# Storing two heads at a time, 64 KB per partition, in a batched Q K^T kernel

## The chip, the cores and the metric

The kernel runs on one core of a Trainium2 chip. The metric is the device time of one execution in microseconds (us). The core has a matrix engine (TensorE, PE in the profile, its weight loads PEld), VectorE (DVE), ScalarE (ACT), GpSimd (POOL) and SyncE (SP, which here only issues transfers). Sixteen transfer engines move data between the main memory (HBM) and the on-chip memory (SBUF, 128 partitions). Transfers are issued by SP (queue q1 of the profile) and by ScalarE (q10), and all of them share the sixteen engines. A transfer is made of packets; each engine closes its part of a transfer with a 4-byte record. TensorE writes only to PSUM, from where ScalarE or VectorE copies to SBUF.

## The reference

For 8 x 12 = 96 heads, each with Q and K of 1024 rows by 64 columns in f32, the kernel computes all products of a row of Q with a row of K:

```python
batch, n_heads, seq, head_dim = 8, 12, 1024, 64
np.einsum('bhid,bhjd->bhij', q, k).astype(np.float32)
```

One head's result is 1024 x 1024 f32, 4 MiB; all 96 are 402.65 MB. Q and K together are 50.33 MB. No softmax and no scaling follow.

## The kernel before

**Blocks.** The 96 heads are cut into blocks of 2, 2, 4, 8, 8 and then six of 12 heads (`sizes`, L33). A block's Q and K are loaded, cast to f16, transposed so that the head dimension lies on the partitions, and then multiplied head by head. All of the work is written in one program order per engine (`pin`), so that each engine's queue runs in the order of the code; engines wait for each other by data only.

**Loads.** For the first three blocks the raw input goes into the first half of what is later an output buffer, `early` (32 KB per partition). From the fourth block on, each block's Q and K go into two buffers of `in_pool` (L73). `next_load` takes the next of these from the list `stream`: two at the start, the rest on ScalarE's queue, both of a block together, after the second eviction of one head of the block two before it (`LOADS`, L263: head 1 of block 2, head 4 of blocks 3 and 4, head 6 otherwise). A load waits until POOL has cast what was in its buffer.

**Cast.** POOL casts f32 to f16 in chunks (`cast_quads`, L127), four instructions of 32 partitions per chunk, into one of five buffers of `half_pool`; `CHUNK` bounds a chunk's columns. Blocks of 8 heads give eight chunks of 1024 columns, blocks of 12 eight chunks of 1536. The first two blocks are cast by `cast_rows` (L97).

**Transpose.** VectorE transposes each chunk in blocks of 32 x 32 into `qT` and `kT` (L145). The first half of a block's heads lies on partitions 0 to 63, the second half on 64 to 127; head n uses half `n // (N/2)` and column group `g = n % (N/2)`. The transposes of the next block are spread over the heads of the present one (`side`), two buffers each of `qT` and `kT` alternate. The first two blocks are transposed by TensorE (L151, copied out at L154).

**Scores.** For one head (`scores`, L156), TensorE multiplies 128 rows of Q by 512 rows of K at a time, over the 64 partitions of the head's half (L171). Row `8 p + t` of the head comes out on partition p for the t-th of eight groups, so that each partition holds eight whole rows of the result, 32 KB that are contiguous in HBM. Two PSUM buffers of 2048 columns alternate; ScalarE copies each to the output buffer (L181), four copies per head; only the first head has copies of 1024 columns, half of them on VectorE (L179). SP then stores the head in one transfer of 4 MiB (L185). There are three output buffers (`out_pool`, L45).

Of the kernel before, what the change touches and what calls it, by code (L numbers as in the profile page):

```python
# [8 lines left out]
F16 = mybir.dt.float16  # L9
F32 = mybir.dt.float32  # L10
P = 128

@with_exitstack
def kernel(
# [6 lines left out]
    nc = tc.nc  # L21

    B, H, S, D = q.shape
    NT = S // P
    BH = B * H
# [4 lines left out]
    kf = k.rearrange("b h s d -> (b h s) d")  # L30
    of = out.rearrange("b h i j -> (b h) i j")

    sizes = [2, 2, 4, 8, 8] + [12] * ((BH - 24) // 12)  # L33
    assert sum(sizes) == BH
    PE_BLOCKS = 2
    NMAX = max(sizes)
    CHUNK = 48 * 32

    consts = ctx.enter_context(tc.tile_pool(name="consts", bufs=1))
    ident = consts.tile([P, P], F16)  # L40

    in_pool = ctx.enter_context(tc.tile_pool(name="in_pool", bufs=2))
    half_pool = ctx.enter_context(tc.tile_pool(name="half_pool", bufs=5))
    tr_pool = ctx.enter_context(tc.tile_pool(name="tr_pool", bufs=2))
    out_pool = ctx.enter_context(tc.tile_pool(name="out_pool", bufs=3))  # L45

    pin = tc.keep_in_program_order

    def half_tile():
        half_sb = half_pool.tile([P, CHUNK], F16, tag="half")  # L50
        return half_sb

    class Block:
# [3 lines left out]
        def __init__(self, first, N, by_pe):  # L57
# [5 lines left out]
            self.halves = {}  # L63
            self.cut = max(1, self.R * 32 // CHUNK + (self.R * 32 % CHUNK > 0))

# [87 lines left out]
            src = t_ps.rearrange("c t m -> c m t")  # L153
            pin(copy(out=dst, in_=src))  # L154

        def scores(self, n, side, ps_pool, w):  # L156

            half, g = divmod(n, self.N // 2)
            cs = slice(half * D, (half + 1) * D)

            qT = self.qT.rearrange("c (g m t) -> c g t m", t=NT, m=P)
            kT = self.kT.rearrange("c (g j) -> c g j", j=S)
            o_sb = out_pool.tile([P, NT, S], F32, tag="out")
            for u in range(NT // w):
                ps = ps_pool.tile([P, w * S], F32, tag="po")
                for tt in range(w):
                    for j in range(2):
                        js = slice(j * 512, (j + 1) * 512)
                        at = tt * S + j * 512
                        pin(  # L170
                            nc.tensor.matmul(  # L171
                                ps[:, at : at + 512],
                                qT[cs, g, w * u + tt],
                                kT[cs, g, js],
                            )
                        )
                dst = o_sb[:, w * u : w * u + w].rearrange("p t j -> p (t j)")
                if w == 1 and u % 2:
                    pin(nc.vector.tensor_copy(out=dst, in_=ps))  # L179
                else:  # L180
                    pin(nc.scalar.copy(out=dst, in_=ps))  # L181
                for do in side.get(u, []):
                    do()
            pin(
                nc.sync.dma_start(  # L185
                    out=of[self.first + n].rearrange("(p t) j -> p (t j)", p=P),
                    in_=o_sb.rearrange("p t j -> p (t j)"),
                )
            )

    blocks, first = [], 0
    for i, N in enumerate(sizes):
        blocks.append(Block(first, N, i < PE_BLOCKS))
        first += N

    early = out_pool.tile([P, NT, S], F32, tag="out")
    raw = early.rearrange("p t j -> p (t j)")
    at = 0
    for b in blocks[:3]:
# [12 lines left out]
    def next_load(eng):  # L212
        if stream:
            b, x = stream.pop(0)
            b.load(x, eng)
# [9 lines left out]
    def to_half(last):  # L225
        while casts:
            i, c = casts[0]
            if i > last or (blocks[i], c[0]) in stream:
                return
            blocks[i].cast_quads(*c)  # L230
            casts.pop(0)

    for b in blocks[:PE_BLOCKS]:
        for x in range(2):
            b.cast_rows(x)
    to_half(2)

    def block(i, heads, ps_pool, w):
        b = blocks[i]
        nxt = blocks[i + 1] if i + 1 < len(blocks) else None  # L240
        for n in heads:
            side = {}
            if nxt and nxt.by_pe:
                if n == 1:
                    side = {
                        u: [
                            lambda x=u // 2: nxt.transpose_rows(
                                x, ps_pool, nc.vector.tensor_copy
                            )
                        ]  # L250
                        for u in (1, 3)
                    }
            elif nxt:
                parts = nxt.chunks()
                some = [s for m, s in enumerate(parts) if m * b.N // len(parts) == n]
                side = {0: [lambda s=s: nxt.transpose_quads(*s) for s in some]}

            if n == LOADS.get(i, 6):
                side[1] = side.get(1, []) + [lambda: next_load(nc.scalar)] * 2
            b.scores(n, side, ps_pool, w)  # L260
            to_half(i + 2 + (n == b.N - 1))

    LOADS = {0: None, 1: None, 2: 1, 3: 4, 4: 4}  # L263

    blocks[0].alloc()
    blocks[1].alloc()
    with tc.tile_pool(name="first_pool", bufs=4, space=bass.MemoryType.PSUM) as pool:
        for x in range(2):
            blocks[0].transpose_rows(x, pool, (nc.vector.tensor_copy, nc.scalar.copy)[x])
        block(0, [0], pool, 1)  # L270
    po_pool = ctx.enter_context(
        tc.tile_pool(name="po_pool", bufs=2, space=bass.MemoryType.PSUM)
    )
    block(0, [1], po_pool, 2)
    for i in range(1, len(blocks)):
        if i + 1 < len(blocks):
            blocks[i + 1].alloc()
        block(i, range(blocks[i].N), po_pool, 2)


# [28 lines left out]
```

## Time and profile before

| what | value |
|---|---|
| median of the runs | 1063.13 us (1063.09 to 1063.64) |
| span of the profiled execution | 1061.8 us (the median of the runs is 1.3 above it) |
| PE, DVE, ACT, POOL busy | 66%, 44%, 66%, 35% of the span |
| transfers, mean rate over the span | 453.25 MB, 427 GB/s |
| stores | 96 of 4096 KB, 21.8 us median from issue to landing |
| eviction of 128 x 2048 f32 on ScalarE | 380, 1869 ns mean |
| chain that ended last | stores 70%, ScalarE 17%, PE 7% |

How to read it: an engine's share of busy time tells whether it could be the bound, and the idle time in front of its instructions, with what ended it, tells for whom it waited. In lines of the order of time, the columns are start, duration, engine, source line, operation, output, input, and in brackets the idle time before it. In the chain of waits they are start and duration. In groups, the mean duration of one stands behind the busy time. Shares of transfer queues are of the time of all sixteen engines.

### The profile page before, as it was taken

How to read it: one execution, taken by the hardware profiler on the slowest of the kernel's cores; microseconds unless marked ns; L12 is line 12 of the kernel's file. 1: busy time of each engine (PE TensorE's matmuls, PEld its weight loads, DVE VectorE, ACT ScalarE, POOL GpSimd, SP SyncE). 2: the span in 40 equal slices, each digit the busy share in tenths (PEclk: the TensorE clock that was granted, in tenths of full speed). 3: DMA queues.
4: the chain of work that ended last, by engine and by line, in shares of the span. 5: the costliest groups of instructions: out<-in, count | busy, mean ns of one | idle time of the engine just before them, and what ended most of it. 6: DMA issues, size and time to landing. Idle time of an engine off the chain costs nothing.

```text
span 1061.8 us, 4282 instructions
## 1 busy us (share of the span) xinstructions
PE 701.3 (66%) x1568; PEld 241.6 (23%) x1568; DVE 471.5 (44%) x75; ACT 697.6 (66%) x386; POOL 368.3 (35%) x286
## 2 busy tenths in 40 slices
PE   6866755755677367773677836777367777778770
PEld 2322211211222122221222212222122222222220
DVE  2999601991696007960079600795007950000000
ACT  4856745755777366774677746777467777777771
POOL 6959128607630463303733046330463200000000
DMA  9999999999999999999999999999999999999997
GB/s 385 428 429 435 433 431 435 435 422 440 428 430 432 432 430 432 435 422 429 431 433 431 415 436 431 433 435 422 428 434 435 434 432 432 434 433 427 434 431 311
DMA packets 17588, 453.25 MB, mean 427 GB/s; under 512 B 1952, under 2 KB 1952, under 8 KB 2976
## 3 DMA queue, kind: packets, MB, share of 16 engines
q1 hardware_dynamic: 14688, 406.85, 89.1%
q10 hardware_dynamic: 2880, 46.14, 10.4%
q8 instruction: 12, 0.20, 0.1%
q14 instruction: 8, 0.07, 0.0%
HBM read 50.33 MB, written 402.65 MB: 427 GB/s over the span
## 4 chain that ended last, share of the span: by engine, by line
DMA 70%; ACT 17%; PE 7%; DVE 2%; issue 1%; POOL 1%; ACTq 0%; SPq 0%
DMA out_dram<-o_sb 70%; ACT o_sb L181 17%; PE ps L171 7%; DVE qT L145 1%; DVE kT L145 1%; DMA early<-in_q_dram 0%; POOL half_sb L127 0%; PE ps L151 0%; POOL half_sb L97 0%; DVE kT L154 0%; DVE o_sb L179 0%; ACTq L181 0%; ACT kT L154 0%; SPq L84 0%; ACTq L73 0%
## 5 line engine op out<-in xcount | busy, mean ns | idle before, releaser
L181 ACT COPY o_sb<-ps 128x2048 f32<-128x2048 f32 (+1 forms) x384 | 695.3, 1860 | 334.7 <-DMA out_dram<-o_sb 298.4
L171 PE MATMUL ps<-kT,qT 64*128 64x512 f16 x1536 | 697.2, 617 | 329.4 <-ACT o_sb L181 325.6
L127 POOL CAST half_sb<-x_sb 32x1536 f16<-32x1536 f32 (+1 forms) x256 | 346.5, 1353 | 455.1 <-DMA x_sb<-in_q_dram 318.3
L171 PEld LDWEIGHTS <-qT 64*128 64x128 f16 x1536 | 238.4, 157 | 786.3 <-issue 781.9
L145 DVE STREAM_TRANSPOSE qT<-half_sb 128x1536 f16<-128x1536 f16 (+1 forms) x34 | 232.8, 7140 | 372.2 <-issue 372.2
L145 DVE STREAM_TRANSPOSE kT<-half_sb 128x1536 f16<-128x1536 f16 (+1 forms) x34 | 234.2, 7181 | 0.0
L127 POOL CAST half_sb<-early 32x1024 f16<-32x1024 f32 x16 | 16.5, 1033 | 4.0 <-DMA early<-in_q_dram 3.3
L151 PE MATMUL ps<-ident,half_sb 128*128 128x128 f16 x32 | 4.1, 309 | 6.7 <-POOL half_sb L97 6.1
L154 DVE COPY qT<-ps 128x1024 f16<-128x1024 f16 x2 | 2.4, 1224 | 12.3 <-PE ps L151 12.3
L179 DVE COPY o_sb<-ps 128x1024 f32<-128x1024 f32 x4 | 4.9, 1224 | 4.3 <-PE ps L171 4.3
L97 POOL CAST half_sb<-early 128x512 f16<-128x512 f32 x8 | 4.6, 613 | 4.1 <-DMA early<-in_q_dram 4.1
L151 PEld LDWEIGHTS <-half_sb 128*128 128x128 f16 x32 | 3.2, 139 | 8.6 <-POOL half_sb L97 6.5
L154 ACT ACT_TABLE_LOAD x1 | 1.3, 1283 | 5.8 <-DMA early<-in_q_dram 5.8
L154 DVE COPY kT<-ps 128x1024 f16<-128x1024 f16 x1 | 1.2, 1224 | 4.3 <-PE ps L151 4.3
L154 ACT COPY kT<-ps 128x1024 f16<-128x1024 f16 x1 | 1.0, 1012 | 1.2 <-PE ps L151 1.2
masks.py:199 POOL TENSOR_SCALAR_AFFINE_SELECT ident<-ident 128x128 f16<-128x128 f16 x1 | 0.3, 292 | 0.1
masks.py:197 POOL MEMSET ident<- 128x128 f16 x1 | 0.2, 204 | 0.3 <-POOLq L293 0.3
L293 POOL MEMSET const-float32-0.0<- 128x1 f32 x1 | 0.1, 98 | 0.2 <-issue 0.2
L293 POOL MEMSET const-uint8-127<- 128x1 uint8 x1 | 0.1, 101 | 0.0
L293 POOL MEMSET const-bfloat16-1.0<- 128x1 bf16 x1 | 0.1, 100 | 0.0
L293 POOL MEMSET const-float32-1.0<- 128x1 f32 x1 | 0.1, 98 | 0.0
## 6 DMA issues: line engine op xcount, KB each, us to landing
out_dram<-o_sb SPq DMA_DIRECT2D x96, 4096.0 KB, 21.8
x_sb<-in_q_dram ACTq DMA_DIRECT2D x6, 3072.0 KB, 22.8
x_sb<-in_k_dram ACTq DMA_DIRECT2D x6, 3072.0 KB, 39.6
x_sb<-in_k_dram ACTq DMA_DIRECT2D x2, 2048.0 KB, 22.2
x_sb<-in_q_dram SPq DMA_DIRECT2D x1, 2048.0 KB, 18.0
x_sb<-in_q_dram ACTq DMA_DIRECT2D x1, 2048.0 KB, 19.0
early<-in_k_dram ACTq DMA_DIRECT2D x4, 256.0 KB, 5.0
early<-in_q_dram SPq DMA_DIRECT2D x4, 256.0 KB, 4.7
```

The source lines that it names most:

```text
L97: nc.gpsimd.tensor_copy(out=self.rows[x][:, :, half], in_=self.raw[x][:, half * n : (half + 1) * n].rearrange("p (r d) -> p r d", d=D),)
L127: nc.gpsimd.tensor_copy(out=half_sb[q0 : q0 + 32].rearrange("p (r d) -> p r d", d=32), in_=raw[32 * b : 32 * b + 32, c * m : (c + 1) * m, h],)
L145: pin(nc.vector.transpose(out=dst, in_=src))
L151: pin(nc.tensor.transpose(t_ps[:, t], self.rows[x][:, t], ident))
L154: pin(copy(out=dst, in_=src))
L171: nc.tensor.matmul(ps[:, at : at + 512], qT[cs, g, w * u + tt], kT[cs, g, js],)
L179: pin(nc.vector.tensor_copy(out=dst, in_=ps))
L181: pin(nc.scalar.copy(out=dst, in_=ps))
L293: nc = _bacc.Bacc("TRN2", target_bir_lowering=False, num_devices=1)
```

## The change

After the first three blocks (heads 0 to 7), two heads of a block are computed and stored together. The heads of a pair are the g-th of the block's first half and the g-th of its second half, which lie on partitions 0 to 63 and 64 to 127 of `qT` and `kT`. VectorE copies Q of both into a tile in which every second column belongs to the other head (`space`): on the partitions of the first head only even columns are filled, on those of the second only odd ones, and the rest is zero from a clear at the start. One matmul over all 128 partitions then gives sixteen-row groups of the first head on the even partitions and of the second on the odd ones (`pair_scores`). Each partition holds 16 rows of one head, 64 KB contiguous in HBM, and one transfer stores both heads, 8 MiB. Two such tiles, used in turn, hold spaced Q.

All blocks from the fourth on have 8 heads, so there are eleven of them, with 44 pairs. There are two output buffers of 64 KB per partition instead of three of 32 KB; the first eight heads, still stored singly, use the four halves of the two. Chunks have at most 1024 columns, and `half_pool` has three buffers instead of five. POOL clears the two spaced tiles behind the casts of block 2. The copies into the spaced tile for the next pair stand in VectorE's order after the first eviction of the present pair, ahead of that pair's share of transposes. The loads of Q and K of a block are no longer issued together but after the third and the seventh eviction of the third pair of the block two before (in block 2, of heads 1 and 3).

```diff
--- before.py
+++ after.py
@@ -30,19 +30,23 @@
     kf = k.rearrange("b h s d -> (b h s) d")
     of = out.rearrange("b h i j -> (b h) i j")
 
-    sizes = [2, 2, 4, 8, 8] + [12] * ((BH - 24) // 12)
+    sizes = [2, 2, 4] + [8] * ((BH - 8) // 8)
     assert sum(sizes) == BH
     PE_BLOCKS = 2
     NMAX = max(sizes)
-    CHUNK = 48 * 32
+    SINGLES = 3
+    CHUNK = 32 * 32
 
     consts = ctx.enter_context(tc.tile_pool(name="consts", bufs=1))
     ident = consts.tile([P, P], F16)
+    spaced_even = consts.tile([P, 2 * NT, D, 2], F16)
+    spaced_odd = consts.tile([P, 2 * NT, D, 2], F16)
+    spaced = [spaced_even, spaced_odd]
 
     in_pool = ctx.enter_context(tc.tile_pool(name="in_pool", bufs=2))
-    half_pool = ctx.enter_context(tc.tile_pool(name="half_pool", bufs=5))
+    half_pool = ctx.enter_context(tc.tile_pool(name="half_pool", bufs=3))
     tr_pool = ctx.enter_context(tc.tile_pool(name="tr_pool", bufs=2))
-    out_pool = ctx.enter_context(tc.tile_pool(name="out_pool", bufs=3))
+    out_pool = ctx.enter_context(tc.tile_pool(name="out_pool", bufs=2))
 
     pin = tc.keep_in_program_order
 
@@ -153,14 +157,13 @@
             src = t_ps.rearrange("c t m -> c m t")
             pin(copy(out=dst, in_=src))
 
-        def scores(self, n, side, ps_pool, w):
+        def scores(self, n, side, ps_pool, w, o_sb):
 
             half, g = divmod(n, self.N // 2)
             cs = slice(half * D, (half + 1) * D)
 
             qT = self.qT.rearrange("c (g m t) -> c g t m", t=NT, m=P)
             kT = self.kT.rearrange("c (g j) -> c g j", j=S)
-            o_sb = out_pool.tile([P, NT, S], F32, tag="out")
             for u in range(NT // w):
                 ps = ps_pool.tile([P, w * S], F32, tag="po")
                 for tt in range(w):
@@ -188,12 +191,58 @@
                 )
             )
 
+        def space(self, g):
+
+            sp = spaced[g % 2].rearrange("c t i s -> c i t s")
+            for s in range(2):
+                cs = slice(s * D, (s + 1) * D)
+                pin(
+                    nc.vector.tensor_copy(
+                        out=sp[cs, :, :, s],
+                        in_=self.qT[cs, g * S : (g + 1) * S].rearrange(
+                            "c (i t) -> c i t", t=2 * NT
+                        ),
+                    )
+                )
+
+        def pair_scores(self, g, side, ps_pool):
+
+            sp = spaced[g % 2].rearrange("c t i s -> c t (i s)")
+            kT = self.kT[:, g * S : (g + 1) * S]
+            o_sb = out_pool.tile([P, 2 * NT, S], F32, tag="out")
+            for u in range(NT):
+                ps = ps_pool.tile([P, 2 * S], F32, tag="po")
+                for tt in range(2):
+                    for j in range(2):
+                        at = tt * S + j * 512
+                        pin(
+                            nc.tensor.matmul(
+                                ps[:, at : at + 512],
+                                sp[:, 2 * u + tt],
+                                kT[:, j * 512 : j * 512 + 512],
+                            )
+                        )
+                dst = o_sb[:, 2 * u : 2 * u + 2].rearrange("p t j -> p (t j)")
+                pin(nc.scalar.copy(out=dst, in_=ps))
+                for do in side.get(u, []):
+                    do()
+            heads = of[self.first : self.first + self.N].rearrange(
+                "(s g) (i t) j -> g i s (t j)", s=2, t=2 * NT
+            )
+            pin(
+                nc.sync.dma_start(
+                    out=heads[g], in_=o_sb.rearrange("p t j -> p (t j)")
+                )
+            )
+
...
-    early = out_pool.tile([P, NT, S], F32, tag="out")
+    singles = out_pool.tile([P, 2 * NT, S], F32, tag="out")
+    early = out_pool.tile([P, 2 * NT, S], F32, tag="out")
+    slots = [singles[:, :NT], singles[:, NT:], early[:, NT:], early[:, :NT]]
     raw = early.rearrange("p t j -> p (t j)")
     at = 0
     for b in blocks[:3]:
@@ -234,6 +283,8 @@
         for x in range(2):
             b.cast_rows(x)
     to_half(2)
+    for sp in spaced:
+        pin(nc.gpsimd.memset(sp, 0.0))
 
     def block(i, heads, ps_pool, w):
         b = blocks[i]
@@ -255,12 +306,37 @@
                 some = [s for m, s in enumerate(parts) if m * b.N // len(parts) == n]
                 side = {0: [lambda s=s: nxt.transpose_quads(*s) for s in some]}
 
-            if n == LOADS.get(i, 6):
-                side[1] = side.get(1, []) + [lambda: next_load(nc.scalar)] * 2
-            b.scores(n, side, ps_pool, w)
+            if i == SINGLES - 1:
+                if n in (1, 3):
+                    side[1] = side.get(1, []) + [lambda: next_load(nc.scalar)]
+                if n == 3:
+                    side[3] = [lambda: nxt.space(0)]
+            b.scores(n, side, ps_pool, w, slots[(b.first + n) % 4])
             to_half(i + 2 + (n == b.N - 1))
 
-    LOADS = {0: None, 1: None, 2: 1, 3: 4, 4: 4}
+    def pair_block(i):
+        b = blocks[i]
+        nxt = blocks[i + 1] if i + 1 < len(blocks) else None
+        pairs = b.N // 2
+        for g in range(pairs):
+            side = {u: [] for u in range(NT)}
+            if g + 1 < pairs:
+                side[0].append(lambda: b.space(g + 1))
+            elif nxt:
+                side[0].append(lambda: nxt.space(0))
+            if nxt:
+                parts = nxt.chunks()
+                side[1] += [
+                    lambda s=s: nxt.transpose_quads(*s)
+                    for m, s in enumerate(parts)
+                    if m * pairs // len(parts) == g
+                ]
+            if g == pairs // 2:
+                side[2].append(lambda: next_load(nc.scalar))
+                side[6].append(lambda: next_load(nc.scalar))
+            b.pair_scores(g, side, ps_pool=po_pool)
+            to_half(i + 2 + (g == pairs - 1))
+
 
     blocks[0].alloc()
     blocks[1].alloc()
@@ -275,7 +351,10 @@
     for i in range(1, len(blocks)):
         if i + 1 < len(blocks):
             blocks[i + 1].alloc()
-        block(i, range(blocks[i].N), po_pool, 2)
+        if i < SINGLES:
+            block(i, range(blocks[i].N), po_pool, 2)
+        else:
+            pair_block(i)
 
 
 # ---- launch: one core; inputs and outputs as the reference has them ----
```

## The prediction

> **What bounds the kernel now.** I read the page's busy shares first, then its rows on transfers, then the chain of waits, then ScalarE's order of time in a stretch without loads, and last the groups kept apart by shape. The page gives shares of the span, the transfer engines in 40 slices, and the two queues that carry data (q1 is SP's, q10 is ScalarE's):
>
> ```profile
> span 1061.8 us, 4282 instructions
> PE 701.3 (66%) x1568; PEld 241.6 (23%) x1568; DVE 471.5 (44%) x75; ACT 697.6 (66%) x386; POOL 368.3 (35%) x286
> DMA  9999999999999999999999999999999999999997
> ...
> q1 hardware_dynamic: 14688, 406.85, 89.1%
> q10 hardware_dynamic: 2880, 46.14, 10.4%
> HBM read 50.33 MB, written 402.65 MB: 427 GB/s over the span
> ```
>
> No compute engine is busy for more than two thirds of the span; the 16 transfer engines are busy 99.5% of it (89.1 + 10.4). ScalarE's order of time, near the end where nothing is loaded, shows who waits for whom:
>
> ```profile
> 885.18 3.63 ACT L181 COPY o_sb<-ps 128x2048 f32<-128x2048 f32 x2 [2.32 <-DMA out_dram<-o_sb]
> 889.00 3.64 ACT L181 COPY o_sb<-ps 128x2048 f32<-128x2048 f32 x2 [0.18 <-PE ps L171]
> 894.97 3.64 ACT L181 COPY o_sb<-ps 128x2048 f32<-128x2048 f32 x2 [2.33 <-DMA out_dram<-o_sb]
> 898.79 3.64 ACT L181 COPY o_sb<-ps 128x2048 f32<-128x2048 f32 x2 [0.17 <-PE ps L171]
> ```
>
> One head is four evictions. They take 7.46 us (885.18 to 892.64), then ScalarE waits 2.32 us for a store to free a buffer: 9.79 us a head. The chain of waits, one round of three heads:
>
> ```profile
> 863.33 21.75 DMA out_dram<-o_sb
> 885.09 0.02 issue
> ...
> 885.18 1.88 ACT o_sb L181
> ...
> 887.10 1.88 PE ps L171 x4
> ...
> 889.00 3.65 ACT o_sb L181 x2
> 892.65 0.02 issue
> 892.67 21.75 DMA out_dram<-o_sb
> ```
>
> A store issued at 863.33 lands at 885.08; 0.1 us later its buffer is refilled, and 892.67 is the next issue: 29.34 us for three heads, 9.78 each. The 21.75 us are mostly queueing, because two other stores are ahead. So the time is what the slowest transfer engine needs for its packets; only a cheaper packet, or a gap in the feed, changes it.
>
> **The packets.** The trace's transfer records give each packet's size and duration. Medians: 2 KB 0.084 us, 8 KB 0.309, 16 KB 0.611, 24 KB 0.912, 32 KB 1.213. From 16 to 32 KB is 0.602 us per 16 KB, so a packet is 37.6 ns per KB plus 9 ns, whatever its size. The 4-byte record that closes a transfer on each engine is 9 ns too. By that line a 64 KB packet would be 2.417 us against 2.426 for two of 32 KB. Other rows bound the 9 ns. Below: the last packets of the slowest engine, when the others have finished, start 1.2095 us apart, 5.3 ns over the 1.2042 of the bytes. Above: 9.78 us a head over 8 packets is 1.2225, 18 ns over, if all of the slowest engine's excess comes per packet. No packet of 64 KB is in the trace. I take 9 ns, which comes from the durations themselves, and keep 5.3 and 18 for the range.
>
> A rule speaks for less. The Trainium skill, page "DMA: Bandwidth & Descriptors", section "Why small descriptors are slow (HBM only)", puts the overhead of a packet at about 3 cycles plus 32 bytes of descriptor data, which with that page's 850 MHz and 27.2 GB/s is, as an estimate, 4.7 ns; by it the sum below would be about -1.8 us instead of -3.1.
>
> **What the change does, part by part.**
> Stores: 88 heads are 704 packets of 32 KB per engine; as 44 pairs they are 352 of 64 KB. 352 x 9 ns = 3.2 us less. 44 fewer store transfers save 44 closing records of 9 ns, 0.4 us.
> Loads: today 16 loads of the streamed blocks (4 of 8 heads, 12 of 12 heads), 128 packets per engine; afterwards 22 loads of 16 KB a partition, 176 packets. 48 x 9 ns and 6 records cost 0.5 us.
> Sum on the transfer engines: -3.1 us (-2.0 with 5.3 ns, -5.8 with 18 ns).
>
> Two buffers for three: this is hidden only while the refill of one 8 MB buffer fits beside the store of the other. The store is 2 x 9.78 = 19.56 us. The refill is eight evictions: 7.46 for the first four, as above, and 7.67 for four in an unbroken run (46.83 to 54.50 in the order of time), 15.1 us. To this come 0.1 from landing to the first eviction and the start of the next transfer: in the first 2.00 us the engines are 18% busy, so they began about 1.64, 0.9 us after the issue at 0.74. Some completion delay lies ahead of the landing; the trace's upper end for all of the latency is the 4.7 us of a whole 256 KB load. So 16.1 to 20.0 us against 19.56. I take about 16.5, as 256 KB needs only a part of that 4.7 to start and land, and the gap is then some 3 us. While loads run, the store takes longer and the gap is wider. Cost: nothing; if the cover goes, ScalarE's eviction pace is late next.
>
> Matmuls: the same number (32 of 512 columns for a pair), now 128 rows deep. Nearest row: the 64-row ones, four in 1.88 us. The 128-row ones on L151 have 128 columns and say nothing of 512. I take 1.88. Up to 2.27 per eviction (18.1 us in eight) would still fit in 19.56 less 1.4.
>
> The zero-spaced copies: two VectorE copies of 64 x 1024 f16 per pair, 88 in all. The groups by shape (busy, mean ns of one) have these neighbours:
>
> ```profile
> L154 DVE COPY qT<-ps 128x1024 f16<-128x1024 f16 x2 | 2.4, 1224 | 12.3 <-PE ps L151 12.3
> L145 DVE STREAM_TRANSPOSE qT<-half_sb 128x1024 f16<-128x1024 f16 x10 | 46.6, 4925 | 1.1 <-issue 1.1
> L127 POOL CAST half_sb<-x_sb 32x1024 f16<-32x1024 f32 x64 | 66.1, 1033 | 13.3 <-DMA x_sb<-in_q_dram 9.6 <-DVE qT L145 0.9
> ```
>
> At 1.22 us, VectorE has 2.4 us of copies and two transposes of 4.94 per pair, 12.3 us; at the upper end, a copy as slow as a transpose, 19.8, still under the 22.0 us that a pair takes with its share of the loads ((4 x 19.56 + 16 x 0.611) / 4). They are queued ahead of the transposes, a full pair before their matmuls, so they cost nothing. The lower end is nothing as well; there is no gain, since no wait on VectorE ends in the chain after 60 us.
>
> Fewer cast buffers (three for five) and two clears on POOL ahead of block 3's casts. By the 128x128 clear (204 ns against 98 for one column) a clear of 2048 columns is about 1.8 us. A chain of three buffers runs at the transposes' 4.9 us a chunk against 4.3 for four casts. Block 3's casts then end at about 76 us instead of 65.8. Behind them on ScalarE's queue stand the loads of block 4: q's issue would wait until about 59 us, k's until 76; each holds ScalarE some 1 to 2 us, against 8.08 today in one wait. By 84 us all eight single heads are issued, some 25 us of stores ahead of the engines. Later, q's and k's issues stand behind the third and seventh eviction of a block's third pair, and POOL's last cast there ends some 6 us before. Cost: nothing, with up to 5 us if a single head waits for POOL (a rival).
>
> Load landing: a load's packet takes turns with the store's. Today 8 x (1.213 + 0.929) = 17.1 us is the step from q's 22.8 to k's 39.6. Afterwards 8 x (2.417 + 0.611) = 24.2 us each; k then lands some 14 us into the next block and is transposed in that block's third pair, 40 us in. Hidden.
>
> Sum: -3.1 us. Against the profiled span 1061.8 that is 1058.7; the median of the runs, 1063.13, lies 1.33 above that span, so 1060.0.
>
> **Rivals.**
> 1. The row is cut into two of 32 KB, or a long packet costs as much a byte as two short ones. For it: nothing here is longer than 32 KB. Against: five sizes lie on one line. The records saved (0.4) and added pay for each other: 1063.1.
> 2. Two buffers starve the engines (the side of slower). It decides when refill and latency pass 19.56 us. At the upper 20.0 each pair without loads loses 0.44 us. Loads fill 48 of a block's 88 us, so two of four pairs in nine blocks, and all eight of the last two: 26 x 0.44 = 11.4 us, 1071.4. Against it: ScalarE waits for stores 298.4 us in all.
> 3. Packets to two heads in turn run slower. Price by the nearest row, loads beside stores: 24 KB means 0.929 against the median 0.912, 2%. 2% of the pairs' 851 us is 17 us: 1077. For it: the slowest engine already pays 13 ns over its undisturbed spacing in the crowd. Against: bytes and engines are the same. The Trainium skill, "DMA: Bandwidth & Descriptors", section "Latency and other measured facts", says that rows at large power-of-two distances in HBM can halve a copy's rate; the two heads are 16 MiB apart, and no run here shows that distance.
> 4. The third head, whose buffer's other half holds raw input, waits for block 2's casts: these end at about 38 us instead of 30.5, the eviction is due at 31.5, some 2 us of stores are queued: 5 us lost, 1065.
>
> **How the numbers follow.** Chances: forecast 0.62, rivals 0.12, 0.11, 0.08 and 0.07. The forecast's own range is 1057.3 to 1061.1. A change under 0.2% (2.1 us, so 1061.0 to 1065.3) can hardly be told from none. Faster: 0.57 of the first case. Same: its remaining 0.05, rival 1's 0.12, 0.03 of rival 4. Slower: the rest, 0.23. The range runs from 1056.8 to 1072: it takes in rivals 1, 2 and 4 and leaves out rival 3 and the tails.
>
> **What would show it.** Packets of 64 KB at about 2.417 us on q1, half as many; ScalarE waiting some 3 us or more per pair for a store, never a store's issue late; all slices of the engines at 9. Slices below 9 in the last 160 us, or ScalarE without waits for stores, mean rival 2; 64 KB packets well over 2.43 us, rival 3; a low slice within the first 60 us, rival 4.

## The result, and the profile after

The changed kernel takes 1079.2 us (median, 1078.84 to 1080.55) against 1063.1: a ratio of 1.0153, with a 95% interval of 1.0139 to 1.0168. It is 16 us slower than the kernel before, where the forecast of 1060.0 had it 3 us faster, and it lies above the range of 1056.8 to 1072. The profiled execution has a span of 1077.1 us, 15.3 more than before.

The page of the changed kernel, in the order of its parts: busy shares, the transfer engines and their rate in 40 slices, the two queues, and four groups (busy, mean ns of one, idle before it):

```profile
span 1077.1 us, 4435 instructions
PE 504.8 (47%) x1568; PEld 175.8 (16%) x1568; DVE 670.6 (62%) x187; ACT 690.1 (64%) x386; POOL 459.1 (43%) x384
...
DMA  9999999999999999998999999999999899999998
GB/s 389 428 428 430 427 419 438 428 421 416 447 402 428 415 431 425 427 427 372 434 447 402 438 433 405 424 429 431 371 433 443 363 428 455 427 431 431 427 428 355
...
q1 hardware_dynamic: 8352, 406.85, 88.3%
q10 hardware_dynamic: 3744, 46.14, 10.2%
...
L226 ACT COPY o_sb<-ps 128x2048 f32<-128x2048 f32 x352 | 632.6, 1880 | 338.2 <-DMA out_dram<-o_sb 309.6
...
L219 PE MATMUL ps<-kT,spaced_even 128*128 128x512 f16 x704 | 220.6, 448 | 266.6 <-ACT o_sb L226 253.1
L200 DVE COPY spaced_odd<-qT 64x1024 f16<-64x1024 f16 x44 | 117.3, 2666 | 166.9 <-PE ps L219 166.2
```

The same row of rates in the kernel before:

```profile
GB/s 385 428 429 435 433 431 435 435 422 440 428 430 432 432 430 432 435 422 429 431 433 431 415 436 431 433 435 422 428 434 435 434 432 432 434 433 427 434 431 311
```

No compute engine is near a bound, and ScalarE waits 309.6 us for stores, so the transfer engines still set the time. But their row of slices is no longer all 9, and the rate, which between the first slice and the last stayed within 415 to 440 GB/s before, falls to 402, 372, 405, 371 and 363 in single slices. The queues carry the same bytes in fewer packets (q1 8352 instead of 14688).

ScalarE's and SP's order of time around the end of a block's second pair and the start of its third (start, duration, engine, line, operation):

```profile
202.92 3.63 ACT L226 COPY o_sb<-ps 128x2048 f32<-128x2048 f32 x2 [6.88 <-DMA out_dram<-o_sb]
...
210.55 7.17 ACT L226 COPY o_sb<-ps 128x2048 f32<-128x2048 f32 x4 [0.18 <-PE ps L219]
217.75 0.54 SPq L233 DMA_DIRECT2D out_dram<-o_sb  x1
222.22 3.63 ACT L226 COPY o_sb<-ps 128x2048 f32<-128x2048 f32 x2 [4.50 <-DMA out_dram<-o_sb]
...
226.11 0.34 ACTq L77 DMA_DIRECT2D x_sb<-in_q_dram  x1
...
232.62 0.33 ACTq L77 DMA_DIRECT2D x_sb<-in_k_dram  x1
```

The refill runs from 202.92 to 217.72, 14.8 us, and its store is issued at once. ScalarE then waits 4.50 us for the other buffer. Read on ScalarE alone, this is the gap that the forecast wanted. The transfer records, which list every packet with its start, duration and size, tell the other half. The 4-byte records that close the store then running end at 217.9 to 218.2 for thirteen of the sixteen engines, at 218.7 and 219.3 for two, and at 221.8 for the last. Thirteen engines had nothing to do from about 218.0 until the first packets of the new store start at 218.95 to 219.1, while the sixteenth still had some 3.6 us of work. It is this last engine that releases the buffer.

The chain of waits over one block, every other store of it (start, duration):

```profile
217.75 27.99 DMA out_dram<-o_sb
...
260.40 32.11 DMA out_dram<-o_sb
...
307.17 28.15 DMA out_dram<-o_sb
```

From issue 217.75 to issue 307.17, one block of 8 heads, are 89.4 us. Four pairs and two loads without loss would be (4 x 8 x 2.418) + (16 x 0.611) = 87.2 us. After the last load the pairs lose nothing; ScalarE's first evictions there are

```profile
921.52 3.63 ACT L226 COPY o_sb<-ps 128x2048 f32<-128x2048 f32 x2 [6.93 <-DMA out_dram<-o_sb]
...
940.84 3.63 ACT L226 COPY o_sb<-ps 128x2048 f32<-128x2048 f32 x2 [4.79 <-DMA out_dram<-o_sb]
...
960.17 3.64 ACT L226 COPY o_sb<-ps 128x2048 f32<-128x2048 f32 x2 [4.79 <-DMA out_dram<-o_sb]
...
979.50 3.63 ACT L226 COPY o_sb<-ps 128x2048 f32<-128x2048 f32 x2 [4.80 <-DMA out_dram<-o_sb]
```

19.33 us apart, against 2 x 9.78 = 19.56 before. So the loss is made where loads run, or shortly after them.

**A balance from the transfer records.** For every kernel I summed over the packets what each took above the undisturbed median of its size (64 KB 2.418 us, 32 KB 1.213, 24 KB 0.912, 16 KB 0.611) and divided by 16: "stretch" of store and of load packets. "Dry" is the mean time in which an engine had no packet up to 12 us before the last one ended, "end" the same in those 12 us. All in us per engine; the last two columns are against the kernel before. The balance is that of the one execution whose trace was kept, which can lie beside the median of the runs (by 5.7 us below it in e3, by 2.4 above it in e2). A ratio stands with its interval. The experiments follow below.

| kernel | median | ratio | store stretch | load stretch | dry | end | sum | span |
|---|---|---|---|---|---|---|---|---|
| before | 1063.1 | | 3.0 | 3.2 | 0.3 | 5.5 | | |
| after | 1079.2 | 1.0153 [1.0139, 1.0168] | 11.8 | 2.0 | 12.2 | 2.5 | +16.5 | +15.3 |
| e1 blocks of 8 | 1066.0 | 1.0023 [1.0012, 1.0034] | 6.4 | 1.7 | 0.2 | 4.9 | +1.2 | +1.5 |
| e15 same, loads apart | 1065.7 | 1.0023 [1.0014, 1.0033] | 6.7 | 1.8 | 0.1 | 4.3 | +1.0 | +1.0 |
| e2 four buffers | 1069.1 | 1.0058 [1.0043, 1.0073] | 6.1 | 1.9 | 1.4 | 10.0 | +7.5 | +7.9 |
| e9 same, loads joined | 1068.9 | 1.0055 [1.0038, 1.0072] | 6.6 | 2.0 | 0.2 | 7.7 | +4.6 | +5.2 |
| e5 two stores, first half early | 1071.8 | 1.0076 [1.0059, 1.0093] | 6.0 | 6.0 | 1.2 | 7.7 | +9.0 | +9.4 |
| e10 same, loads joined | 1067.1 | 1.0031 [1.0020, 1.0042] | 6.7 | 2.3 | 0.2 | 5.6 | +2.8 | +3.5 |
| e12 two stores, both late | 1072.0 | 1.0084 [1.0067, 1.0101] | 11.4 | 2.1 | 4.6 | 2.3 | +8.4 | +8.4 |
| e13 same, loads joined | 1074.9 | 1.0102 [1.0076, 1.0127] | 10.0 | 6.1 | 3.8 | 1.5 | +9.6 | +10.0 |
| e8 after, loads joined | 1072.7 | 1.0085 [1.0070, 1.0101] | 7.0 | 10.0 | 2.9 | 2.5 | +10.5 | +9.2 |
| e4 after, loads on SP | 1073.8 | 1.0096 [1.0064, 1.0128] | 7.5 | 10.0 | 3.0 | 2.7 | +11.3 | +10.0 |
| e3 short refill | 1092.6 | 1.0267 [1.0233, 1.0301] | 14.8 | 3.5 | 13.5 | 5.0 | +24.9 | +23.3 |
| e14 same, loads joined | 1080.1 | 1.0158 [1.0141, 1.0175] | 10.1 | 7.4 | 6.5 | 5.4 | +17.4 | +16.1 |
| e11 before, loads on SP | 1066.3 | 1.0026 [1.0016, 1.0035] | 1.3 | 4.6 | 0.1 | 8.3 | +2.4 | +2.5 |

The balance closes to within 1.6 us for every kernel. The changed kernel's engines lose 8.8 us more in stretched store packets and 11.9 more in dry spells; they give back 3.0 at the end, where they now finish closer together, and 1.2 on load packets. Dry engines and the slowest engine are two sides of one thing: the others stood dry because the next store had to wait for the buffer that the slowest engine had not yet finished. Of the store stretch, 10.0 us lie in packets that overlap in time with a load packet and 1.8 in the others.

### The profile page after: what moved, and what is told of

The parts are those of the page before. It is cut to its first block, busy times and chain, and to the rows that moved or that the text cites. A ratio compares the mean times of both kernels' runs of the same rounds, so it can differ in the third digit from the quotient of the medians.

```text
span 1077.1 us, 4435 instructions
## 1 busy us (share of the span) xinstructions
PE 504.8 (47%) x1568; PEld 175.8 (16%) x1568; DVE 670.6 (62%) x187; ACT 690.1 (64%) x386; POOL 459.1 (43%) x384
## 3 DMA queue, kind: packets, MB, share of 16 engines
q1 hardware_dynamic: 8352, 406.85, 88.3%
q10 hardware_dynamic: 3744, 46.14, 10.2%
## 4 chain that ended last, share of the span: by engine, by line
DMA 63%; ACT 26%; PE 7%; issue 1%; ACTq 0%; DVE 0%; POOL 0%; SPq 0%
DMA out_dram<-o_sb 57%; ACT o_sb L226 24%; PE ps L219 5%; DMA out_dram<-early 3%; DMA out_dram<-singles 2%; PE ps L174 2%; ACT singles L184 1%; ACT early L184 1%; DMA early<-in_q_dram 0%; PE ps L155 0%; ACTq L383 0%; POOL half_sb L101 0%; DVE kT L158 0%; DVE singles L182 0%; ACT kT L158 0%
## 5 line engine op out<-in xcount | busy, mean ns | idle before, releaser
L226 ACT COPY o_sb<-ps 128x2048 f32<-128x2048 f32 x352 | 632.6, 1880 | 338.2 <-DMA out_dram<-o_sb 309.6
L131 POOL CAST half_sb<-x_sb 32x1024 f16<-32x1024 f32 x352 | 433.7, 1232 | 471.9 <-DMA x_sb<-in_q_dram 236.9
L219 PE MATMUL ps<-kT,spaced_odd 128*128 128x512 f16 x704 | 222.2, 451 | 263.1 <-ACT o_sb L226 263.1
L219 PE MATMUL ps<-kT,spaced_even 128*128 128x512 f16 x704 | 220.6, 448 | 266.6 <-ACT o_sb L226 253.1
L200 DVE COPY spaced_odd<-qT 64x1024 f16<-64x1024 f16 x44 | 117.3, 2666 | 166.9 <-PE ps L219 166.2
L149 DVE STREAM_TRANSPOSE qT<-half_sb 128x1024 f16<-128x1024 f16 x46 | 214.4, 4852 | 1.6 <-POOL half_sb L131 0.9
L149 DVE STREAM_TRANSPOSE kT<-half_sb 128x1024 f16<-128x1024 f16 x46 | 214.3, 4854 | 0.6
L200 DVE COPY spaced_even<-qT 64x1024 f16<-64x1024 f16 x44 | 117.9, 2681 | 155.2 <-PE ps L219 154.5
L174 PE MATMUL ps<-kT,qT 64*128 64x512 f16 x128 | 57.9, 620 | 8.3 <-ACT singles L184 3.0
L184 ACT COPY singles<-ps 128x2048 f32<-128x2048 f32 (+1 forms) x16 | 25.9, 1654 | 10.5 <-PE ps L174 8.8
L174 PEld LDWEIGHTS <-qT 64*128 64x128 f16 x128 | 19.6, 157 | 44.8 <-issue 40.5
L131 POOL CAST half_sb<-early 32x1024 f16<-32x1024 f32 x16 | 16.5, 1034 | 12.1 <-PE ps L155 6.3
```

The lines of the kernel that those rows point to most:

```text
L131: nc.gpsimd.tensor_copy(out=half_sb[q0 : q0 + 32].rearrange("p (r d) -> p r d", d=32), in_=raw[32 * b : 32 * b + 32, c * m : (c + 1) * m, h],)
L149: pin(nc.vector.transpose(out=dst, in_=src))
L174: nc.tensor.matmul(ps[:, at : at + 512], qT[cs, g, w * u + tt], kT[cs, g, js],)
L200: nc.vector.tensor_copy(out=sp[cs, :, :, s], in_=self.qT[cs, g * S : (g + 1) * S].rearrange("c (i t) -> c i t", t=2 * NT),)
L219: nc.tensor.matmul(ps[:, at : at + 512], sp[:, 2 * u + tt], kT[:, j * 512 : j * 512 + 512],)
```

## The experiments

**Blocks of 8 heads alone (e1).** Single heads and three buffers as before, but the block sizes and chunks of the change.

```diff
-    sizes = [2, 2, 4, 8, 8] + [12] * ((BH - 24) // 12)
+    sizes = [2, 2, 4] + [8] * ((BH - 8) // 8)
-    CHUNK = 48 * 32
+    CHUNK = 32 * 32
-            if n == LOADS.get(i, 6):
+            if n == LOADS.get(i, 4):
...
-    LOADS = {0: None, 1: None, 2: 1, 3: 4, 4: 4}
+    LOADS = {0: None, 1: None, 2: 1}
```

> The kernel before with one thing of the change: blocks of 8 heads throughout (chunks of 1024 columns, 16 KB load packets, both loads of a block together at its fifth head). Heads stay single, 32 KB packets, three buffers. Theory L (each start of loads beside stores costs the engines a fixed loss, and there are ten such starts instead of six, with Q and K apart twenty): most of the 16 us return, 1070 to 1077 us. Theory S (the two large buffers come back too late for the engines that are ahead of the slowest one): three small buffers stay ahead, so 1063 to 1066. Theory P (64 KB packets interleave badly with loads): 1063 to 1066 as well.

1066.0 us. The smaller blocks cost about 2.5 us, most of it stretch of the store packets (3.0 to 6.4): there are eleven load phases instead of eight (ten and seven without the first block loaded this way; the expectation's "six" is one short). The rest of the 16 us, 13.2, belongs to the pairs.

**Pairs from four buffers of 32 KB (e2).** Each pair is stored as two transfers, each from a buffer of its own that is issued after four evictions and released by itself.

```diff
-    out_pool = ctx.enter_context(tc.tile_pool(name="out_pool", bufs=2))
+    out_pool = ctx.enter_context(tc.tile_pool(name="out_pool", bufs=4))
...
+                if u % 4 == 0:
+                    o_sb = out_pool.tile([P, NT, S], F32, tag="out")
...
+                if u % 4 == 3:
+                    pin(nc.sync.dma_start(out=heads[g, u // 4], ...))
```

> The changed kernel with each pair stored as two transfers of 32 KB per partition, out of four buffers of 32 KB instead of two of 64 KB. Pairs, spaced Q, blocks of 8 and the places of the loads are as in the changed kernel. Theory S: a buffer of half the size comes back after four evictions and three others are ahead, so the engines never run dry: 1062 to 1066 us. Theory P: 1062 to 1066 too, since no packet is over 32 KB. Theory L: the loads start as often as in the changed kernel, 1074 to 1079.

1069.1 us, between the ranges of the three theories: 10 us of the 16 are gone with the same matmuls, copies and loads. So they lie in how the result is buffered and stored.

**A shorter refill (e3).** The matmuls and evictions of the last two of eight steps of each pair are left out, so a quarter of those outputs is not computed; the store is as large as before.

```diff
+                if u < 6:
                     ps = ps_pool.tile([P, 2 * S], F32, tag="po")
...
-            o_sb = out_pool.tile([P, 2 * NT, S], F32, tag="out")
+            o_sb = outs[g % 2]
```

> The changed kernel with the matmuls and evictions of the last quarter of each pair left out (six of eight evictions of 2048 columns; the stored rows of that quarter hold older data). All transfers, packets, loads and buffers are unchanged; only the refill shortens from 14.5 to about 10.8 us. Theory S: the engines ahead no longer run dry, their idle 12 us and the lockstep after it go, and the cheaper packets show: 1058 to 1064 us. Theory L or P: nothing that they name changes, 1075 to 1080 us.

1092.6 us, 13 us more than with the full refill and outside every range expected. If the engines merely starved for want of an earlier store, this would have cured it; that theory falls. The closing records show the engines 6 to 11 us apart here once the loads of the pair blocks run, and mostly 3.5 to 5 in the changed kernel (up to 7.4). The engines ahead ran further ahead with the extra room, and were dry again (13.5 us).

**Loads on SP's queue (e4), and both loads together (e8).**

```diff
# e4
-                side[2].append(lambda: next_load(nc.scalar))
-                side[6].append(lambda: next_load(nc.scalar))
+                side[2].append(lambda: next_load(nc.sync))
+                side[6].append(lambda: next_load(nc.sync))
# e8
-                side[2].append(lambda: next_load(nc.scalar))
+                side[6].append(lambda: next_load(nc.scalar))
```

> The changed kernel with the loads of the pair blocks issued on SP's queue instead of ScalarE's: they stand in line between two stores and no longer take turns with a store's packets. Theory P or L (the loss is made where loads and stores take turns): the lengthened packets go, 1060 to 1066 us. Theory S: the load fills the gap in front of one store in four, the one where most idle time was seen, but the others then have no loads beside them that stretch them, so part stays: 1066 to 1075 us.

> The changed kernel with both loads of a block issued together after the seventh eviction of the third pair, as the kernel before issues them together. Theory L in its weaker form (every start of loads on an idle queue stretches the packets of all engines by about 0.6 us): ten starts less, 1072 to 1075 us. Theories P and S2: the loads take as many turns, 1077 to 1081.

1073.8 and 1072.7 us. Both cut the dry time from 12.2 to 3 us. But the stretch only changes sides: store packets 11.8 to 7.5 and 7.0, load packets 2.0 to 10.0. Even with the loads in the store's own queue, store and load packets together are stretched by 17.5 us.

**Packets of 32 KB from the same two buffers (e5).**

```diff
-                "(s g) (i t) j -> g i s (t j)", s=2, t=2 * NT
+                "(s g) (i h t) j -> g h i s (t j)", s=2, h=2, t=NT
...
+            for h in range(2):
                 pin(
                     nc.sync.dma_start(
-                        out=heads[g], in_=o_sb.rearrange("p t j -> p (t j)")
+                        out=heads[g, h],
+                        in_=o_sb[:, h * NT : (h + 1) * NT].rearrange("p t j -> p (t j)"),
                     )
                 )
```

> The changed kernel with the same two buffers of 64 KB, but each pair is stored by two transfers of 32 KB per partition, both issued after the last eviction. Only the packet size (and 44 more transfers) differs. Theory P (the long packets are what suffers beside loads): the loss goes although the buffers are as before, 1066 to 1071 us, near the 1069 of the four small buffers. Theory S2 (two buffers that come back as a whole let the engines ahead run dry and start again in step, and those out of step pay in the load phases): nothing is gained and the cheaper packets are lost, 1077 to 1084.

1071.8 us, just above the range of theory P. At first I read this as the price of the 64 KB packet, 7.4 us. But the edit did more than it was meant to do. In the variant with joined loads, SP's order of time has the first half leave after four evictions, 7.1 us ahead of the second:

```profile
897.31 0.54 SPq L234 DMA_DIRECT2D out_dram<-o_sb  x1
...
904.39 0.54 SPq L234 DMA_DIRECT2D out_dram<-o_sb  x1
```

**Without the loads (e6 pairs, e7 single heads).** Blocks 5 to 13 are computed from the raw data of block 4 (e6 from the changed kernel, e7 from e1).

```diff
-    stream = [(b, x) for b in blocks[3:] for x in range(2)]
+    stream = [(b, x) for b in blocks[3:5] for x in range(2)]
...
+            if blocks[i].raw[c[0]] is None:
+                blocks[i].raw[c[0]] = blocks[4].raw[c[0]]
```

> The changed kernel without the loads of blocks 5 to 13; their heads are computed from block 4's input, so only heads 0 to 15 are the reference's. From about 100 us on, only stores run. To be compared with the singles in the next run. If all of the loss is made beside loads (theories P and S2), the pairs run at the 19.36 us seen at the end of the changed kernel and end 3 to 10 us ahead of the singles. If two buffers cost time by themselves, they end behind the singles.

> The kernel with single heads in blocks of 8 (first experiment), without the loads of blocks 5 to 13 in the same way; only heads 0 to 15 are the reference's. 18 loads of 4.9 us fall away: 1066 less 88 is 978, and up to 6 us less if packets stretched by loads go too: 972 to 978.

975.0 us for pairs, 976.3 for single heads. First the page's lines of e6, then of e7 (queue, packets, MB, share):

```profile
span 973.4 us, 4381 instructions
...
q1 hardware_dynamic: 8352, 406.85, 97.0%
q10 hardware_dynamic: 1152, 8.39, 2.1%
```

```profile
span 974.5 us, 4382 instructions
...
q1 hardware_dynamic: 14688, 406.85, 97.1%
q10 hardware_dynamic: 1152, 8.39, 2.1%
```

Without loads the pairs are 1.3 us ahead, as a saving of records would have it, though less than the 3 to 10 expected. With them they are 13.2 us behind (1079.2 against e1's 1066.0). The whole loss of the pairs needs the loads. Dry time by itself is not the loss: in e6 the engines are dry for some 4 us more than in e7, but they also end some 4 us closer together, and the time does not grow.

**Joined loads with the other buffers (e9, e10), and single heads with loads apart (e15).** e9 is e2 and e10 is e5, each with the edit of e8; e15 is e1 with the second load one head later.

> As the pairs out of four buffers of 32 KB per partition (1069.1 us), but with both loads of a block together after the seventh eviction of the third pair. Theory L+P (separate losses that add: loads apart instead of together, and packets of 64 KB beside loads): it gains as much as joining gained with whole pairs (6.5 us), 1062 to 1065, the mean idle time of the engines stays under 1.5 us. Theory of one loss only (joining helps by shrinking the dry spells of two large buffers, of which four small ones have none to lose): no gain, 1068 to 1070.

> As the two 64 KB buffers stored by two transfers of 32 KB per partition (1071.8 us), loads together. Separate losses that add: 1064 to 1067. One loss only (a transfer engine that falls behind in load phases, whichever change helps it first): 1070 to 1072, as little below 1071.8 as the joined loads are below 1072.7.

> Blocks of 8 heads with single heads and three buffers (1066.0 us), with a block's two loads one head apart (four evictions, as in the changed kernel) instead of together. If loads apart cost only with large buffers: 1065 to 1068. If they cost the slowest transfer engine the same everywhere (6.5 us with 64 KB, 4.7 us with 32 KB halves): 1070 to 1073.

1068.9, 1067.1 and 1065.7 us. Joining gains 6.5 us with whole pairs and 4.7 in e10, but 0.2 with four buffers, and with single heads loads apart cost nothing. The two disagree on what was to be told apart: e9 lies in the range for one loss only, e10 at the edge of that for separate losses that add. e10 is the best kernel with two large buffers. Its page:

```profile
span 1065.3 us, 4564 instructions
...
DMA  9999999999999999999999999999999999999997
GB/s 373 432 433 431 431 431 431 433 427 429 433 432 425 435 433 421 435 432 423 424 433 431 425 429 432 427 430 432 424 427 433 433 415 435 432 433 432 432 433 304
```

The slices are at 9 again, and after the first slice none but the last is below 415 GB/s.

**Both halves late (e12, and e13 with joined loads).** As e5 and e10, but the second half first, so that both transfers stand behind the eighth eviction. Now the packet size alone differs from the changed kernel and from e8.

```diff
-            for h in range(2):
+            for h in (1, 0):
```

> The two transfers of 32 KB per partition again (1071.8 us), but the second half of the buffer is stored first. With the first half first, the trace shows its issue 7.1 us before the other (897.31 and 904.39 us in the kernel with joined loads), since it waits for only four evictions. Now both stand behind the eighth eviction, as the one transfer of 64 KB does. If the packets' size made the 7.4 us between the changed kernel and that variant: 1071 to 1073, engines dry for 1 to 2 us. If the earlier issue of the first half made it: 1077 to 1081, engines dry for 9 to 13 us ahead of the last stores.

> The same with the loads of a block together. Packets' size: 1066 to 1068, as with the first half first (1067.1). Earlier issue: 1071 to 1075, as with packets of 64 KB and joined loads (1072.7), engines dry for some 3 us.

1072.0 and 1074.9 us (the four runs of the latter from 1070.2 to 1076.5). With loads apart, the smaller packets alone are worth 7.2 us and the early half another 0.2. These 7.2 us are dry time (12.2 against 4.6, more than the 1 to 2 expected), not stretch. With joined loads the early half is worth 7.8 and the smaller packets nothing (1074.9 against 1072.7, with ranges that overlap). e12 also shows that the stretch of the store packets does not need 64 KB: it is 11.4 us with 32 KB, nearly as large as the 11.8 in the changed kernel.

**Short refill with joined loads (e14).** e3 with the edit of e8.

> Whole pairs in packets of 64 KB, the matmuls and evictions of the last quarter of each pair left out (that quarter of the outputs is not computed), and the loads of a block together. Room alone does not help (1092.6 us with the loads apart). If packets of 64 KB do no harm of their own, and room helps only once the loads come together (as the earlier first half gained 7.8 us with joined loads and nothing with loads apart): 1064 to 1068, the dry time under 1 us. If packets of 64 KB beside loads harm by themselves: 1072 to 1085, the stretch of the store packets 7 us and more.

1080.1 us: the second of the two outcomes. Read as the expectation has it, packets of 64 KB do harm beside loads even where the refill is early and the loads come together. That is argued and not shown: the nearest kernel with 32 KB packets, e10 (1067.1 us), also issues its first half earlier, and no run has a short refill with 32 KB packets. ScalarE's and SP's order of time in e14:

```profile
402.87 3.63 ACT L227 COPY singles<-ps 128x2048 f32<-128x2048 f32 x2 [8.29 <-DMA out_dram<-singles]
...
413.94 0.54 SPq L234 DMA_DIRECT2D out_dram<-singles  x1
...
425.52 3.63 ACT L227 COPY early<-ps 128x2048 f32<-128x2048 f32 x2 [11.60 <-DMA out_dram<-early]
```

The store leaves 11.1 us after its buffer came free, 3.7 earlier than at 14.8, and ScalarE waits 8 to 12 us. By the closing records the engines are 6 to 9 us apart.

**The kernel before with its later loads on SP (e11).** One edit, `nc.scalar` to `nc.sync` in its `next_load`, as a version that might beat both.

> The kernel before with its later loads in SP's queue, between two stores, instead of ScalarE's. If the loss beside loads comes from load packets taking turns with store packets of another queue, the 32 KB packets lose their 3.0 us of stretch and the time falls to 1060 to 1062. If the loss only moves from the store's packets to the load's, as it did with pairs (64 KB packets 7.3 us, 16 KB packets 9.4 us over their undisturbed times): 1062 to 1068, the 24 KB packets stretched by more than the 1.6 us they have now.

1066.3 us, slower by 0.26%. The store packets lose their stretch (3.0 to 1.3), the load packets take it over (3.2 to 4.6), and the engines end further apart (8.3 instead of 5.5). No kernel tried beats the one before.

## Why the prediction was wrong

**The bound** was read rightly: the last transfer engine's packets set the time, in both kernels.

**The packet.** 64 KB take 2.418 us, forecast 2.417. The saving was put too high. In the balance, the five kernels with 64 KB packets lie 1.2 to 1.6 us in span below what stretch and dry time explain (mean 1.3), the eight with pairs or blocks of 8 in 32 KB packets 0.0 to 0.7 above (mean 0.35, which is the load records that were forecast at 0.5). The difference, 1.7 us over 352 packets, is 4.8 ns a packet, with the 44 closing records saved counted in (3.7 ns if these alone saved their 0.4 us): near the forecast's lower end of 5.3, not the 9 of the durations. The last pairs, where nothing is loaded, agree: the slowest engine's closing records stand 19.32 us apart there, 2.414 a packet, 5 ns less than two starts of 1.2095. In the records a packet starts some 3 ns before the one ahead of it ends, which the durations do not show. The sum should have been near -1.3 us, if the length of the packets mattered nowhere else. But beside loads it did: with one transfer of 64 KB packets in place of two late ones of 32 KB (e12 against the changed kernel), and the loads apart, the time grew by 7.2 us, and no term of the forecast allowed for that. The Trainium skill's page "DMA: Bandwidth & Descriptors", section "Why small descriptors are slow (HBM only)", from which 4.7 ns were estimated, agrees with these 3.7 to 4.8 ns and was the better price.

**"Two buffers for three ... Cost: nothing"** is the step that failed. Its own numbers came out: refill 14.8 us (forecast 15.1), 1.65 us of latency (about 1.4 taken), a gap of some 3 us. (Its upper end of 20.0 adds up to 19.9.) But the gap was set against one landing. A buffer is released by the slowest of sixteen engines, and the next store must be issued before the fastest of them has finished. The room for their spread is 19.33 (store of the other buffer) - 14.83 (refill) - 0.45 (from the last closing record, 221.77, to ScalarE's first eviction, 222.22) - 1.2 (from the issue, 217.75, to the first packet, 218.95) = 2.85 us. The spread that the closing records show in the last, undisturbed pairs is 2.7 to 3.0. The same sum fits the others: 19.33 - 11.07 - 1.65 = 6.6 for the short refill (6.2 to 6.5 measured at the end of e14), and 19.33 - 7.48 - 1.65 = 10.2 for the early first half, issued 7.48 us after the first eviction (9.6 in e10). In the kernel before, with three buffers, it is 2 x 9.78 - 7.46 - 1.65 = 10.5, and the spread, which grows from 0.6 to 8.0 us over the run with up to 10.5 beside loads, just fits: 0.3 us dry. The forecast could have read that spread from the trace. But the room says only how far apart the engines can drift, not what the time will be: e12 and e8 have the room of the changed kernel and are dry for 4.6 and 2.9 us instead of 12.2, and with more room than it e3 is slower. What the runs show is that two buffers cost nothing without loads (e6), and that beside loads four small ones take back 10 of the 13.2 us (e2).

While loads run, a store takes 21 to 27 us by its closing records, so the room is wider and the spread grows, mostly to between 3.7 and 5 us. When the store of a block's second pair is issued (217.75), the loads have ended (their last packet at 188.0); the store ahead of it takes 19.3 us again, the room is back at 2.85, the spread still 3.85, and the engines ahead stand dry for the difference: that is why dry spells stand at 218.0, 307.0, 396.3 and so on, in every block. I had named "slices below 9 in the last 160 us" as the sign of rival 2, and looked for the loss where nothing is loaded; it is where loads have just ended.

**The loads** are the second mis-sized term: 0.5 us for records, "hidden" otherwise. They also stretch the stores beside them: store and load packets together are stretched by 13.8 us in the changed kernel, 6.2 before. When q is issued at 226.11 on an idle queue, the fourteen packets of 64 KB that start from 228.68 to 228.83 all take 0.57 to 0.60 us longer.

**What the two add up to.** Not a sum. Going from e1 to the changed kernel, by single steps after the first, gives 1066.0, 1067.1 (pairs, large buffers, halves; loads joined as in e1), 1071.8 (loads apart), 1072.0 (both halves late), 1079.2 (one packet of 64 KB); by another path, 1067.1, 1074.9 (both late), 1072.7 (64 KB), 1079.2 (apart). What can be said: blocks of 8 cost 2.5 us; loads apart cost nothing without the large buffers; with two large buffers, loads apart alone (e5) or a late store alone (e13) bring the time to 1072 to 1075, as does either with one more of the three (e12, e8), and late store, loads apart and 64 KB packets together to 1079.

**Open** stays why packets beside loads are stretched by 8 us in one kernel and by 17 in another. Engines in step with each other (late store) go with stretch even at 32 KB, but e14 has its engines 6 to 9 us apart and 17.5 us of stretch. That 64 KB packets of engines out of step meet bursts of load packets is an argument, not shown.

**Beside the path**, all as forecast or without effect: the 128-row matmuls take 448 to 451 ns, less than the 470 taken. The spaced copies take 2.67 us instead of 1.22, within their upper end; VectorE is 62% busy and hides them, but for one wait of 13.3 us of TensorE ahead of the first pair, in which no engine ran dry. The clears take 1.80 us each, and block 4's loads are issued at 59.4 and 76.7 us (forecast 59 and 76).

**The rivals.** 1 did not occur: the packet is on the line. 2 named the right kind, engines run dry by two buffers, but with 0.44 us a pair in pairs without loads it had the wrong place and price. 3 came nearest in time (1077), by luck, for its mechanism was the wrong one: two heads in turn run at full speed when nothing is loaded (19.33 us a pair). 4 did not occur; the third head's first eviction is at 31.45 us.

## What to carry to other kernels

When buffers become larger and fewer, compare the room between refill and store not with zero but with the spread of the transfer engines, which the closing records of the stores show: here room is the store time of the other buffers, less the refill up to the issue, less 1.65 us, and the engines of the kernel before were up to 10.5 us apart. A transfer that is issued as soon as its part of a buffer is full keeps that room without a further buffer; here it paid with the loads joined (e10 against e13, 7.8 us) and not with the loads apart (e5 against e12, 0.2). Price a larger packet by differences of start times, not of durations, and price it beside the loads it will meet.

## What the runs showed of the hardware

- The sixteen engines of one core drift apart although each has the same packets: 8 us at the end of the kernel before, 9.4 in e10. The Trainium skill's page "DMA: Bandwidth & Descriptors", section "Why a DMA increments its semaphore by 16 and not by 1", says that they finish independently; by how much, only the records show.
- Engines that run dry pull together, and thirteen of them then finish a store within 0.3 us (217.9 to 218.2).
- More room can cost time: 3.7 us less refill made the kernel 13 us slower with loads apart and 7 us slower with loads joined (e3 against after, e14 against e8).
- TensorE's granted clock fell from 1.00 to a mean of 0.79 with matmuls of 128 rows. ScalarE waited 9.7 us in all for the matmuls of pairs (24.9 for those of the heads before), so no cost of it is seen.
